# Mixer C: the rounded weight copies move from ScalarE to GpSimd

## The chip, the cores and the metric

The kernel runs on one core of one Trainium2 chip. The core's engines run side by side, each with its own instruction queue, in order: TensorE (PE, with its weight loads as PEld), VectorE (DVE), ScalarE (ACT), GpSimd (POOL) and SyncE (SP), which issues most DMAs. The metric is the device time of one execution in microseconds; smaller is better. Times of several runs are compared by their median.

## The reference

One inference step of a two-layer backbone on 128 context and 1024 latent tokens, 1152 in all, 1024 wide. The even layer has a windowed attention and a bidirectional recurrence side by side; the odd layer, mixer C, is differential attention with 8 heads:

```
h = rms_norm(x, norm_pre) * (1.0 + scale) + shift
qc, kc, vc, gc = split_cols(h @ w_in, ...)        # 8 heads of 128 columns each
p = softmax(q . k / 8)  for both halves of a head # keys: context cache and latent tokens
att = p[0] - lam * p[1]
o = rms_norm(att @ v, subln) * (1.0 - lam_init)
y = (o * silu(gc)) @ w_out
x = x + gate * rms_norm(y, norm_post)
```

Context tokens see context tokens only. Outputs are both token groups and new caches. Everything is fp32.

## The kernel before, in words

To keep fp32 accuracy with TensorE's rounded fp32 format, each operand of a matmul is held as a rounded copy (`hi`) and the remainder (`lo` = value minus `hi`), and a product is three matmuls: hi by hi, lo by hi, hi by lo. For weights this is `load_split` (L265): for each tile of `step` columns SyncE loads `raw` by DMA (L269), ScalarE writes the rounded copy `hi` (L270), and GpSimd writes `lo` = `raw` - `hi` (L271). `weights` (L379) makes the two buffers and calls it.

In the layer of mixer C the tokens lie in nine tiles of 128. For each head h, `c_project` (L1491) loads the head's projection weights `wc` (1024 x 384, six tiles of 128 x 512, buffers `wch` and `wcl`), then for each token tile does 24 matmuls (L360 with `wch`, L361 with `wcl`, L362 with `wch` and the tokens' remainder), rotates q and k (VectorE makes `ropea` and `ropeb`, GpSimd adds them to q and k, L407), casts v, and turns k by a TensorE transpose (L1519) into the key buffer `kst`. `c_probs` makes a token tile's scores `s` (L1555), their minimum `mx` over the negated scores on VectorE (L1557, L1559), the exponentials `p` on ScalarE (L1562) and the difference of the two halves on VectorE (L1575). `c_values` turns that difference (L1593), splits it into `ah` (ScalarE) and `al` (VectorE) and multiplies by v (L1603 to L1605). `c_query` turns and splits q into `qs` (L1533, L1535, L1536). `c_gate` is the gate path (L1620 to L1622), with gate weights `wg` (1024 x 128, two tiles of 128 x 512) that `gate_weights` (L1772) loads; `c_norm` normalizes and multiplies by the gate.

The heads overlap: while head h attends, `ahead` projects head h + 1. Its last part, the first 19 steps of the head after that (`EARLY`), is begun in the last group of head h. There is one buffer of `wch` and one of `wcl` (pool `wc`, one buffer), so a new head's copies wait until TensorE has done the last projection matmul of the head before. There are two buffers of `raw` in the layer (pool `rc`), which also carry the cached keys and values. Head 0's weights are loaded earlier, while the even layer ends, from other `raw` buffers. The generators are interleaved by `zipped` and `run`, and the framework's scheduler then sets the order of each engine's queue by its own costs; the program's text gives the priorities. An engine takes its instructions in that order and waits at each for its inputs.

Of the kernel before, what the change touches and what calls it, by code (L numbers as in the profile page):

```python
# [19 lines left out]
P = 128  # L20
D = 1024
KT = D // P
NT = 9
TOK = NT * P
THIRD = 384
# [116 lines left out]
def hybrid_step(ctx: ExitStack, tc: tile.TileContext, I, O, stop=99):  # L142
    nc = tc.nc
    PE, VE, AE, GE, SP = nc.tensor, nc.vector, nc.scalar, nc.gpsimd, nc.sync
# [7 lines left out]
    def space(name, bufs, **kw):  # L152
        return tc.tile_pool(name=name, bufs=bufs, reuse_waits="tile", **kw)
# [3 lines left out]
    def tl(pool, shape, tag, dt=F32, bufs=None):  # L157
        uid[0] += 1
        kw = {} if bufs is None else {"bufs": bufs}
        return pool.tile(list(shape), dt, tag=tag, name=f"{tag}_{uid[0]}", **kw)  # L160
# [101 lines left out]
        VE.scalar_tensor_tensor(y, t, 1.5, y, op0=ALU.add, op1=ALU.mult)  # L262
        return y

    def load_split(src, hi, lo, n, raw_pool, step=1024, eng=GE):  # L265
        for j in range(0, n, step):
            w = min(step, n - j)
            raw = tl(raw_pool, [P, step], "raw")
            SP.dma_start(raw[:, :w], src[:, j:j + w])  # L269
            AE.copy(hi[:, j:j + w], raw[:, :w])  # L270
            eng.tensor_tensor(lo[:, j:j + w], raw[:, :w], hi[:, j:j + w].bitcast(F32), ALU.subtract)  # L271


# [83 lines left out]
    def proj_steps(ps, hh, hl, wh, wl, t, n):  # L357
        s = slice(P * t, P * t + P)
        for k in range(KT):
            PE.matmul(ps[:, :n], hh[:, k, s], wh[:, k], start=k == 0, stop=False)  # L360
            PE.matmul(ps[:, :n], hh[:, k, s], wl[:, k], start=False, stop=False)  # L361
            PE.matmul(ps[:, :n], hl[:, k, s], wh[:, k], start=False, stop=k == KT - 1)  # L362
            yield
# [12 lines left out]
                PE.matmul(ps[:, :THIRD], wl[:, k], hh[:, k, s], start=False, stop=k == KT - 1)  # L376
            yield i, ps

    def weights(pool, src, n, tag, raw_pool, step=1024, bufs=None):  # L379
        hi, lo = (tl(pool, [P, KT, n], tag + e, F32R, bufs) for e in "hl")  # L380
        load_split(src.rearrange("p k n -> p (k n)"), hi.rearrange("p k n -> p (k n)"),
                   lo.rearrange("p k n -> p (k n)"), KT * n, raw_pool, step)
        return hi, lo

    def rope_apply(pool, rope, ps, n, t, outs):


        w = 64 * n
        m = n // len(outs)
        twice = lambda v, i: v[:, 64 * m * i:64 * m * i + 64 * m].rearrange("p (h o d) -> p h o d", o=1, d=64).to_broadcast(  # L390
            [P, m, 2, 64])
        if t is None:
            for i, out in enumerate(outs):
                AE.copy(out, twice(ps, i))
            return
        cos, sin = rope[:, 0, t], rope[:, 1, t]
        a, b = tl(pool, [P, w], "ropea"), tl(pool, [P, w], "ropeb")
        VE.tensor_tensor(a.rearrange("p (h d) -> p h d", d=64), ps[:, :w].rearrange("p (h d) -> p h d", d=64),
                         cos.rearrange("p (o d) -> p o d", o=1).to_broadcast([P, n, 64]), ALU.mult)
        pv = ps[:, :w].rearrange("p (h c s d) -> p h c s d", c=2, s=2, d=16)  # L400
        bv = b.rearrange("p (h c s d) -> p h c s d", c=2, s=2, d=16)
        sv = sin.rearrange("p (o c s d) -> p o c s d", o=1, c=2, s=2)
        for s in range(2):
            VE.tensor_tensor(bv[:, :, :, s], pv[:, :, :, 1 - s], sv[:, :, :, s].to_broadcast([P, n, 2, 16]),  # L404
                             ALU.mult)
        for i, out in enumerate(outs):
            GE.tensor_tensor(out, twice(a, i), twice(b, i), ALU.add)  # L407
# [15 lines left out]
    def stack_split(dst, src):  # L423
        AE.copy(dst, src)
        VE.tensor_tensor(dst[64:], src[64:], dst[64:].bitcast(F32), ALU.subtract)
# [269 lines left out]
    with ExitStack() as ph1:  # L695
# [35 lines left out]
        rp = ph1.enter_context(space("rp", 2))  # L731
        wq = ph1.enter_context(space("wq", 2))
        wp = ph1.enter_context(space("wp", 2))
# [28 lines left out]
    class Out:  # L762
# [6 lines left out]
        def load_first(s, pool, raw=None, eng=VE):  # L769

            for k in range(4):
                if k in (0, 3):
                    tag, n = ("wg", P) if k else ("wc", THIRD)
                    views = [tl(pool, [P, KT, n], tag + e, F32R).rearrange("p k n -> p (k n)") for e in "hl"]
                hi, lo = (v[:, D * (k % 3):D * (k % 3) + D] for v in views)
                s.w.append((hi, lo))
                for c in (0, 512):
                    load_split(I["wo"][s.l][:, k, c:c + 512], hi[:, c:c + 512], lo[:, c:c + 512], 512, raw or s.raw, 512,
                               eng)
                    yield  # L780

        def load(s, n):

            k0 = len(s.w)
            p = s.pools.enter_context(space(f"ow{s.l}{k0}", 1, side="right"))
            for k in range(k0, k0 + n):
                hi, lo = tl(p, [P, D], f"wo{k}h", F32R), tl(p, [P, D], f"wo{k}l", F32R)
                load_split(I["wo"][s.l][:, k], hi, lo, D, s.raw, 512, VE)
                s.w.append((hi, lo))
# [482 lines left out]
    with ExitStack() as ph2:  # L1272
        bc = ph2.enter_context(space("bc", 1))
        pool = ph2.enter_context(space("bpool", 1))
        last = ph2.enter_context(space("b2", 1))
        early = ph2.enter_context(ExitStack())
        first = ph2.enter_context(ExitStack())
# [91 lines left out]
        for i in range(-2, len(items)):  # L1369
# [16 lines left out]
            if i + 2 == len(items):  # L1386
                run(mod, 1, None, 1)
                first.close()
                wp = late.enter_context(space("wc", 1, side="right"))
# [47 lines left out]
    def split(hi, lo, src):  # L1437
        AE.copy(hi, src)  # L1438
        VE.tensor_tensor(lo, src, hi.bitcast(F32), ALU.subtract)  # L1439
# [7 lines left out]
    def c_open(h, hd, rp, ap):  # L1447

        hd.kst = tl(ap, [P, 2, TOK], "kst", F32R)
        hd.sums = tl(ap, [P, 2 * NT], "sums")  # L1450
        hd.vh, hd.vl = tl(ap, [P, NT, P], "vh", F32R), tl(ap, [P, NT, P], "vl", F32R)
        hd.kp = tl(ap, [P, 2, P], "kp", F32R, 1)
        hd.vph, hd.vpl = tl(ap, [P, P], "vph", F32R, 1), tl(ap, [P, P], "vpl", F32R, 1)
        raw = tl(rp, [P, 512], "raw")
        kr, vr = raw[:, 0:2 * P].rearrange("p (z n) -> p z n", z=2), raw[:, 2 * P:3 * P]
        SP.dma_start(kr, I["ckT"][h])
        SP.dma_start(vr, I["cv"][:, h])
        stack_split(hd.kst[:, :, 0:P], kr)
        split(hd.vh[:, 0], hd.vl[:, 0], vr)
# [30 lines left out]

    def c_project(h, hd, hh, hl, wp, rp, ap, psum, rope):  # L1491
        p_pr, p_tr, p_s, p_o = psum
        wh, wl = weights(wp, I["wc"][h], THIRD, "wc", rp, 512)
        c_open(h, hd, rp, ap)
        yield
        keys = None
        for t in range(NT):
            ps = tl(p_pr, [P, 512], "ps")
            for i, _ in enumerate(proj_steps(ps, hh, hl, wh, wl, t, THIRD)):
                if i == KDEL and keys:  # L1500
                    keys()
                yield
            q, k = tl(ap, [P, 2, 2, 64], "q", bufs=10), tl(ap, [P, 2, 2, 64], "k")
            rope_apply(ap, rope, ps, 4, None if t == 0 else t - 1, (q, k))
            hd.q[t] = q
            if t == 0:
                v = tl(rp, [P, 512], "raw")[:, :P]
                VE.tensor_copy(v, ps[:, 256:384])
                for z in range(2):
                    SP.dma_start(O["ck"][:, h, 64 * z:64 * z + 64], k[:, z, 0])  # L1510
                SP.dma_start(O["cv"][:, h], v)
                split(hd.vph, hd.vpl, v)
            else:
                split(hd.vh[:, t], hd.vl[:, t], ps[:, 256:384])

            def keys(t=t, k=k):
                pt = tl(p_tr, [P, 2, P], "pt")
                for i in range(2):
                    PE.transpose(pt[:, i], k[:, i].rearrange("p o d -> p (o d)"), ident)  # L1519
                stack_split(hd.kp if t == 0 else hd.kst[:, :, P * t:P * t + P], pt)  # L1520

            yield
        for _ in range(KDEL):
            yield
        keys()
        yield
# [153 lines left out]
    with ExitStack() as ph3:  # L1680
# [79 lines left out]
        rp = ph3.enter_context(space("rc", 2))  # L1760
# [4 lines left out]
        heads = [Head() for _ in range(8)]  # L1765

        def project(h):
            if h == 0:
                return c_restore(heads[0], rp, ap, psum)
            return c_project(h, heads[h], hh, hl, wp, rp, ap, psum, rope) if h < 8 else None  # L1770

        def gate_weights(h):  # L1772
            heads[h].wg = weights(wp, I["wgc"][h], P, "wg", rp, 512)

        def gates(h):
            gate_weights(h)
            for _ in range(9):
                yield
            for i in range(3):
                yield from c_gate(i, heads[h], hh, hl, ap, psum)  # L1780
# [28 lines left out]
        first = w1.load_first(wp, rp, GE)  # L1809
# [78 lines left out]
```

## Time and profile before

| what | us |
|---|---|
| median of 3 runs (lowest, highest) | 2082.01 (2075.63, 2087.13) |
| span of the profiled execution | 2077.4 |
| TensorE busy, of the span | 1952.1 |
| VectorE busy | 1488.3 |
| ScalarE busy | 1058.8 |
| GpSimd busy | 673.6 |

The page gives no time around the span. The stretch of mixer C in which the heads' weights are made is about 1170 to 1895 us of the span. A timeline row reads: start, length, engine, line, operation, output from inputs, shape, count, and in brackets how long the engine was idle before it and what ended that idle time. In a row of one source line the three numbers are minimum, median and maximum in ns.

### The profile page before, as it was taken

How to read it: one execution, taken by the hardware profiler on the slowest of the kernel's cores; microseconds unless marked ns; L12 is line 12 of the kernel's file. 1: busy time of each engine (PE TensorE's matmuls, PEld its weight loads, DVE VectorE, ACT ScalarE, POOL GpSimd, SP SyncE). 2: the span in 40 equal slices, each digit the busy share in tenths (PEclk: the TensorE clock that was granted, in tenths of full speed). 3: DMA queues.
4: the chain of work that ended last, by engine and by line, in shares of the span. 5: the costliest groups of instructions: out<-in, count | busy, mean ns of one | idle time of the engine just before them, and what ended most of it. 6: DMA issues, size and time to landing. Idle time of an engine off the chain costs nothing. (4 is left out here: it accounts for less than half of the span.)

```text
span 2077.4 us, 40804 instructions
## 1 busy us (share of the span) xinstructions
PE 1952.1 (94%) x15148; PEld 1777.4 (86%) x15148; DVE 1488.3 (72%) x3821; ACT 1058.8 (51%) x2808; POOL 673.6 (32%) x951
## 2 busy tenths in 40 slices
PE   7899999999789999999989999999999999999998
PEld 7899999999678888777768888999998989898786
DVE  5355567565767787877488587878787878787867
ACT  4343345333446555564356554565555555555643
POOL 0222232332167657575043223121312121212204
PEclk9999999999999999999999999999999999999999
DMA  7511133112555454534576401010101010101325
GB/s 290 163 62 65 61 98 115 63 57 78 181 178 158 146 171 148 157 111 129 167 228 218 133 21 45 15 50 10 51 9 55 6 56 5 55 5 49 106 68 177
DMA packets 165079, 205.72 MB, mean 99 GB/s; under 512 B 16368, under 2 KB 108048, under 8 KB 164880
## 3 DMA queue, kind: packets, MB, share of 16 engines
q1 hardware_dynamic: 162016, 198.25, 30.1%
q10 hardware_dynamic: 2864, 4.85, 0.7%
q8 instruction: 120, 1.97, 0.4%
q14 instruction: 79, 0.65, 0.1%
HBM read 152.32 MB, written 50.74 MB: 98 GB/s over the span
## 5 line engine op out<-in xcount | busy, mean ns | idle before, releaser
L1562 ACT ACTIVATE p<-s,mx 128x384 f32<-128x384 f32 (+1 forms) x400 | 225.1, 572 | 123.0 <-DVE mx L1559 100.3
L1557 DVE TENSOR_REDUCE mc<-s 128x1 f32<-128x384 f32 x384 | 204.4, 551 | 29.3 <-PE s L1555 26.2
L1555 PE MATMUL s<-kst,qs 128*128 128x384 f32 x768 | 196.0, 355 | 14.1 <-ACT p L1562 13.6
L360 PE MATMUL ps<-wch,hh 128*128 128x384 f32 x576 | 205.5, 358 | 3.0 <-DMA raw<-in_wgc_dram 0.9
L361 PE MATMUL ps<-wcl,hh 128*128 128x384 f32 x576 | 198.6, 345 | 4.1 <-POOL wcl L271 4.1
L362 PE MATMUL ps<-wch,hl 128*128 128x384 f32 x576 | 196.4, 341 | 0.3 <-DVE hl L1707 0.2
L407 POOL TENSOR_TENSOR q<-ropea,ropeb 128x256 f32<-128x256 f32 x56 | 44.0, 786 | 442.4 <-DVE ropeb L404 302.3
L374 PE MATMUL ps<-hh,wgh 128*128 128x384 f32 x504 | 174.5, 346 | 5.8 <-DVE bo L242 4.3
L376 PE MATMUL ps<-hh,wgl 128*128 128x384 f32 x504 | 172.4, 342 | 0.0
L375 PE MATMUL ps<-hl,wgh 128*128 128x384 f32 x504 | 171.9, 341 | 0.0
L1555 PEld LDWEIGHTS s<-kst,qs 128*128 128x128 f32 x768 | 127.5, 190 | 29.8 <-ACT p L1562 22.4
L271 POOL TENSOR_TENSOR wgl<-raw,wgh 128x1024 fp32r<-128x1024 f32 (+1 forms) x39 | 75.5, 1939 | 234.5 <-ACT wgh L270 234.5
L1083 POOL TENSOR_TENSOR rp<-rp,tmp 128x126 f32<-128x126 f32 (+22 forms) x279 | 130.3, 467 | 21.9
L1081 POOL TENSOR_TENSOR tmp<-mp,rp 128x126 f32<-128x126 f32 (+22 forms) x279 | 117.8, 422 | 52.3 <-DVE mp L1072 31.1
L1438 ACT CAST ah<-pt 128x512 fp32r<-128x512 f32 (+2 forms) x168 | 86.1, 533 | 79.7 <-PE pt L1593 76.3
L1439 DVE TENSOR_TENSOR al<-pt,ah 128x512 fp32r<-128x512 f32 (+2 forms) x168 | 100.6, 615 | 32.1 <-ACT ah L1438 30.8
L360 PEld LDWEIGHTS ps<-wch,hh 128*128 128x128 f32 x576 | 109.6, 191 | 6.5 <-DVE vl L1439 2.4
L361 PEld LDWEIGHTS ps<-wcl,hh 128*128 128x128 f32 x576 | 109.8, 191 | 6.2 <-POOL wcl L271 5.8
L362 PEld LDWEIGHTS ps<-wch,hl 128*128 128x128 f32 x576 | 109.5, 190 | 1.4 <-DVE hl L1707 1.3
L271 POOL TENSOR_TENSOR wcl<-raw,wch 128x512 fp32r<-128x512 f32 x54 | 76.5, 1423 | 84.5 <-ACT wch L270 84.5
L374 PEld LDWEIGHTS ps<-hh,wgh 128*128 128x128 f32 x504 | 95.4, 189 | 8.1 <-DVE bo L242 4.9
L1575 DVE SCALAR_TENSOR_TENSOR p<-p,lr,p 128x1152 f32<-128x1152 f32 (+1 forms) x72 | 98.4, 1367 | 0.4
(463 smaller groups left out, 5721.7 us busy)
## 6 DMA issues: line engine op xcount, KB each, us to landing
hb<-pbT SPq DMA_DIRECT2D x90, 256.0 KB, 3.9
adaw<-in_ada_w_dram SPq DMA_DIRECT2D x56, 256.0 KB, 3.6
raw<-in_wc_dram SPq DMA_DIRECT2D x48, 256.0 KB, 2.7
adaw<-in_ada_w_dram SPq DMA_DIRECT2D x8, 1024.0 KB, 10.9
pbT<-bm SPq DMA_DIRECT2D x16, 512.0 KB, 2.7
low<-lowT SPq DMA_DIRECT2D x16, 512.0 KB, 4.1
raw<-in_wo_dram SPq DMA_DIRECT2D x32, 256.0 KB, 2.8
raw<-in_wpb_dram SPq DMA_DIRECT2D x13, 512.0 KB, 3.4
```

The costliest lines, as they stand in the source:

```text
L271: eng.tensor_tensor(lo[:, j:j + w], raw[:, :w], hi[:, j:j + w].bitcast(F32), ALU.subtract)
L360: PE.matmul(ps[:, :n], hh[:, k, s], wh[:, k], start=k == 0, stop=False)
L361: PE.matmul(ps[:, :n], hh[:, k, s], wl[:, k], start=False, stop=False)
L362: PE.matmul(ps[:, :n], hl[:, k, s], wh[:, k], start=False, stop=k == KT - 1)
L374: PE.matmul(ps[:, :THIRD], wh[:, k], hh[:, k, s], start=k == 0, stop=False)
L375: PE.matmul(ps[:, :THIRD], wh[:, k], hl[:, k, s], start=False, stop=False)
L376: PE.matmul(ps[:, :THIRD], wl[:, k], hh[:, k, s], start=False, stop=k == KT - 1)
L1081: eng.tensor_tensor(tv, m[:, j - a:j - a + 1, 0:j].to_broadcast([P, n, j]), rpb[:, t:16, j:j + 1].to_broadcast([P, n, j]), ALU.mult)
L1083: eng.tensor_tensor(rpb[:, t:16, 0:j], rpb[:, t:16, 0:j], tv, ALU.add)
L1555: PE.matmul(s[c][:, :w], qs[:, e, z], hd.kp[:, z] if own else hd.kst[:, z, w * c:w * c + w], start=e == 0, stop=e == 1)
L1557: VE.tensor_reduce(mc[:, c:c + 1] if nb > 1 else mx, s[c][:, :w], axis=AX.X, op=ALU.min)
L1562: AE.activation(e[:, w * c:w * c + w], s[c][:, :w], AF.Exp, scale=-1.0, bias=mx, accum_out=sums[:, z, c:c + 1])
```

## The change

`load_split` and `weights` take a function `first` that writes the rounded copy; without it ScalarE does so as before. The projection weights of heads 1 to 7 and the gate weights of heads 1 to 7 are given `GE.tensor_copy`, GpSimd's copy.

```
-    def load_split(src, hi, lo, n, raw_pool, step=1024, eng=GE):
+    def load_split(src, hi, lo, n, raw_pool, step=1024, eng=GE, first=None):
...
-            AE.copy(hi[:, j:j + w], raw[:, :w])
+            (first or AE.copy)(hi[:, j:j + w], raw[:, :w])
...
-    def weights(pool, src, n, tag, raw_pool, step=1024, bufs=None):
+    def weights(pool, src, n, tag, raw_pool, step=1024, bufs=None, first=None):
...
-                   lo.rearrange("p k n -> p (k n)"), KT * n, raw_pool, step)
+                   lo.rearrange("p k n -> p (k n)"), KT * n, raw_pool, step, first=first)
...
-        wh, wl = weights(wp, I["wc"][h], THIRD, "wc", rp, 512)
+        wh, wl = weights(wp, I["wc"][h], THIRD, "wc", rp, 512, first=GE.tensor_copy)
...
-            heads[h].wg = weights(wp, I["wgc"][h], P, "wg", rp, 512)
+            heads[h].wg = weights(wp, I["wgc"][h], P, "wg", rp, 512, first=GE.tensor_copy)
```

The scheduler also sets a new order on TensorE, VectorE and ScalarE; SyncE's is unchanged. Three places, all where head 3's projection weights (`wch_16697`, `wcl_16698`) take the place of head 2's, in the order of the instructions, with - for before and + for the change. On GpSimd:

```order
 L407 TENSOR_TENSOR q_16349<-ropea_16351,ropeb_16352 128x256
 L407 TENSOR_TENSOR k_16350<-ropea_16351,ropeb_16352 128x256
+L270 CAST wch_16697<-raw_16699 128x512
+L270 CAST wch_16697<-raw_16703 128x512
 L271 TENSOR_TENSOR wcl_16698<-raw_16699,wch_16697 128x512
 L271 TENSOR_TENSOR wcl_16698<-raw_16703,wch_16697 128x512
 L407 TENSOR_TENSOR q_16439<-ropea_16441,ropeb_16442 128x256
 L407 TENSOR_TENSOR k_16440<-ropea_16441,ropeb_16442 128x256
+L270 CAST wch_16697<-raw_16707 128x512
 L271 TENSOR_TENSOR wcl_16698<-raw_16707,wch_16697 128x512
```

Two copies stand ahead of the two subtractions and so ahead of the rotated q and k (`k_16440`) of the last token tile of the head before; the other four stand each ahead of its own subtraction. On ScalarE at the same place:

```order
 L424 CAST kst_15384<-pt_16416 128x2x128
-L270 CAST wch_16697<-raw_16699 128x512
-L270 CAST wch_16697<-raw_16703 128x512
 L1438 CAST vh_15386<-ps_16360 128x128
 L1625 ACTIVATE gt_16465<-ps_16426 128x384
-L270 CAST wch_16697<-raw_16707 128x512
 L1438 CAST ah_16474<-pt_16469 128x512
 L1438 CAST ah_16483<-pt_16478 128x512
-L270 CAST wch_16697<-raw_16711 128x512
 L424 CAST kst_15384<-pt_16490 128x2x128
 L1535 ACTIVATE qs_16522<-pt_16519 128x256
-L270 CAST wch_16697<-raw_16715 128x512
```

The copies stood between the casts of turned attention (`ah`), keys and queries; those now follow one another. On TensorE at that place, with the scores `s_3090` and `s_3091` and the transpose of `k_16440`:

```order
-L1622 MATMUL ps_16495<-hh_12964,wgl_15804 128x384
-L1555 MATMUL s_3090_16500<-kst_14181,qs_16330 128x384
 L1603 MATMUL po_16468<-ah_16474,vh_14183 128x256
 L1604 MATMUL po_16468<-ah_16474,vl_14184 128x256
-L1555 MATMUL s_3090_16500<-kst_14181,qs_16330 128x384
-L1555 MATMUL s_3091_16501<-kst_14181,qs_16330 128x384 x2
+L1622 MATMUL ps_16495<-hh_12964,wgl_15804 128x384
+L1555 MATMUL s_3090_16500<-kst_14181,qs_16330 128x384 x2
 L1605 MATMUL po_16468<-al_16475,vh_14183 128x256
 L1519 MATMUL pt_16490<-cst_61,k_16440 128x128 x2
+L1555 MATMUL s_3091_16501<-kst_14181,qs_16330 128x384 x2
```

The value matmuls that read `ah` and the transpose of k stand two to four matmuls earlier than before, and a score block that stood ahead of them now stands behind.

## The prediction

> **What bounds the kernel now.** I read the page first, then the busy times by stretch, then the groups of the stretch in which the change acts, and last the timelines of single places.
>
> ```profile
> PE 1952.1 (94%) x15148; PEld 1777.4 (86%) x15148; DVE 1488.3 (72%) x3821; ACT 1058.8 (51%) x2808; POOL 673.6 (32%) x951
> ```
>
> The page's first part: the columns are busy time, share of the span, count. TensorE is busy for 94% of the span and ScalarE for half of it, so taking work off ScalarE pays only where TensorE waits for it. One head of mixer C repeats about every 102 us, and this is its row:
>
> ```profile
> 1353.00:1455.00 102.00, 99.75 (x637) 94.15 (x637) 82.56 (x235) 58.68 (x176) 24.04 (x24) 1.00 0.10 31
> ```
>
> The columns are length, then busy time of TensorE, its weight loads, VectorE, ScalarE and GpSimd, then the granted clock, the DMA share and GB/s. TensorE is idle for 2.25 of 102 us at full clock. ScalarE has 43 us to spare in it, GpSimd 78. The groups of the stretch 1170 to 1830 us, where seven heads' weights are made, say who ends TensorE's idle time (the last column), and what the moved work costs now:
>
> ```profile
> L361 PE MATMUL ps<-wcl,hh 128*128 128x384 f32 x468 | 161.7, 345 | 4.1 <-POOL wcl L271 4.1
> L1555 PE MATMUL s<-kst,qs 128*128 128x384 f32 x607 | 155.9, 354 | 10.1 <-ACT p L1562 9.5 <-ACT qs L1535 0.5
> L1603 PE MATMUL po<-ah,vh 128*128 128x256 f32 x216 | 70.4, 326 | 2.4 <-ACT ah L1438 2.3
> ...
> L271 POOL TENSOR_TENSOR wcl<-raw,wch 128x512 fp32r<-128x512 f32 x42 | 59.4, 1420 | 73.8 <-ACT wch L270 73.8
> ...
> L270 ACT CAST wch<-raw 128x512 fp32r<-128x512 f32 x42 | 25.4, 623 | 14.5 <-DMA raw<-in_wc_dram 14.4
> ```
>
> So what can be won here is at most 10.1 + 4.1 + 2.4 = 16.6 us of TensorE's idle time, 0.8% of the kernel. What can be lost is not bounded in that way.
>
> **The change part by part.** 42 copies of projection weights (seven heads, six tiles) and 14 of gate weights (seven heads, two tiles) go from ScalarE to GpSimd. ScalarE sheds 56 x 0.623 = 34.9 us of work and, more important, 14.5 us during which its whole queue stood behind a copy whose DMA had not landed. GpSimd gains 56 copies. No SyncE instruction moves. The price of one copy on GpSimd is not in the trace; the nearest row is a copy of the same length per lane on a quarter of the partitions:
>
> ```profile
> L1067 POOL COPY hb<-za x36: 599/610/1007, 578.7 to 946.7; 32x512 f32<-32x512 f32 x36
> ```
>
> It takes 0.61 us (minimum, median, maximum in ns). Above stands the two-input subtraction of 128x512, 1.42 us on average in the group row. I take 0.61, since the length per lane is the same and the input count too; 0.60 and 1.42 stay as ends. The Trainium skill ("GPSIMD Engine Reference", 4.1 Engine selection) calls GpSimd about twice as slow as VectorE for two inputs and roughly line-rate for one input; at its 1.2 GHz and one element a cycle that would be an estimated 0.43 us, and by it k below would come up to 0.36 us earlier at each of six switches, 2.2 us in all. The measured row is slower than the rule; the row is used.
>
> A GpSimd copy does not run undisturbed beside VectorE:
>
> ```profile
> 578.70 3.28 POOL L1067 COPY hb<-za 32x512 f32<-32x512 f32 x4 [14.91 <-DVE za L1040]
> ...
> 579.41 1.08 DVE L988 TENSOR_TENSOR hb<-hb,hb 128x512 f32<-128x512 f32 x1
> 580.52 0.98 DVE L990 TENSOR_TENSOR kbt<-hb,hb 128x512 f32<-128x512 f32 x1
> ```
>
> Four copies took 3.28 instead of 4 x 0.61 = 2.44 us, while VectorE operations on two SBUF operands ran beside them at 1.0 to 1.1 us. I charge this nothing on average, because VectorE has 19 us to spare in a head, and keep it for a rival.
>
> Head 1 (its projection weights are the first that move). The six DMAs begin, the first copy, the first and last subtraction and TensorE's two waits are these:
>
> ```profile
> 1178.65 14.48 SPq L269 DMA_DIRECT2D raw<-in_wc_dram  x6
> 1183.36 0.61 ACT L270 CAST wch<-raw 128x512 fp32r<-128x512 f32 x1
> 1184.04 1.28 POOL L271 TENSOR_TENSOR wcl<-raw,wch 128x512 fp32r<-128x512 f32 x1 [20.20 <-ACT wch L270]
> 1196.51 2.35 POOL L271 TENSOR_TENSOR wcl<-raw,wch 128x512 fp32r<-128x512 f32 x1 [0.24 <-ACT wch L270]
> 1196.33 0.44 PE L361 MATMUL ps<-wcl,hh 128*128 128x384 f32 x1 [0.56 <-POOL wcl L271]
> 1198.91 0.44 PE L361 MATMUL ps<-wcl,hh 128*128 128x384 f32 x1 [1.63 <-POOL wcl L271]
> ```
>
> ```profile
> raw<-in_wc_dram SPq DMA_DIRECT2D x48, 256.0 KB, 2.7
> ```
>
> Here the copies stood between exponentials in ScalarE's queue. On GpSimd a tile takes 0.61 + 1.28 = 1.89 us; with two raw buffers and 2.7 us for a DMA, two tiles take the longer of 3.8 and 1.9 + 2.7 = 4.6. From 1183.4 the fifth tile is done at 1183.4 + 9.2 + 1.9 = 1194.5 and the sixth at 1196.4, against 1198.9 now. TensorE asks for the fifth at 1195.8. Both waits go: **-2.2 us**.
>
> Head 2 is the only other one in which TensorE needs the new weights at once:
>
> ```profile
> 1267.92 1.16 ACT L270 CAST wch<-raw 128x512 fp32r<-128x512 f32 x2
> 1268.64 2.51 POOL L271 TENSOR_TENSOR wcl<-raw,wch 128x512 fp32r<-128x512 f32 x2 [3.52 <-ACT wch L270]
> 1273.67 0.69 PE L1519 MATMUL pt<-cst,k 128*128 128x128 f32 x2 [1.85 <-POOL k L407]
> 1284.32 0.44 PE L361 MATMUL ps<-wcl,hh 128*128 128x384 f32 x1 [0.58 <-POOL wcl L271]
> ```
>
> The copies can begin when TensorE has left the old weights, at 1267.9 in both kernels. Now the subtraction follows 0.72 us later; then it follows two copies, 1.22 us later. All that GpSimd has behind it, the two subtractions and the rotated q and k, is **0.5 us later**, and TensorE waits for k. The third to sixth copies no longer stand behind ScalarE's `ah`, so the 0.58 at 1284 goes. Sum -0.1.
>
> Heads 3 to 7. TensorE has gate matmuls to do and asks for the new weights at 1377, some 19 us after the first copy, so the chain of copies is hidden. What counts is the queue behind them:
>
> ```profile
> 1358.18 1.14 ACT L270 CAST wch<-raw 128x512 fp32r<-128x512 f32 x2
> 1363.48 1.07 ACT L1438 CAST ah<-pt 128x512 fp32r<-128x512 f32 x2
> 1369.00 0.59 ACT L1562 ACTIVATE p<-s,mx 128x384 f32<-128x384 f32 x1
> 1358.87 3.69 POOL L271 TENSOR_TENSOR wcl<-raw,wch 128x512 fp32r<-128x512 f32 x2 [4.10 <-ACT wch L270]
> 1363.23 0.72 POOL L407 TENSOR_TENSOR k<-ropea,ropeb 128x256 f32<-128x256 f32 x1
> 1364.11 0.39 PE L1603 MATMUL po<-ah,vh 128*128 128x256 f32 x1 [0.58 <-ACT ah L1438]
> 1365.11 0.38 PE L1519 MATMUL pt<-cst,k 128*128 128x128 f32 x2
> 1369.73 0.62 PE L1555 MATMUL s<-kst,qs 128*128 128x384 f32 x2 [0.41 <-ACT p L1562]
> 1377.31 0.34 PE L360 MATMUL ps<-wch,hh 128*128 128x384 f32 x1
> ```
>
> With no copy ahead of it, `ah` comes about 1 us earlier and the 0.58 goes. But k, done at 1363.95 now, is done at 1364.5, and the new order has TensorE at the k transpose (L1519) about 1.1 us earlier than 1365.1: it would wait about 0.5 there. Likewise p comes some 0.7 us earlier, but the new order asks for its score matmul five matmuls, about 0.7 us, earlier. I book **0** for these five heads.
>
> Gate weights. Here ScalarE's queue stands behind a DMA, worst in the later heads:
>
> ```profile
> 1602.88 0.62 ACT L270 CAST wgh<-raw 128x512 fp32r<-128x512 f32 x1 [1.47 <-DMA raw<-in_wgc_dram]
> 1604.34 0.58 ACT L1562 ACTIVATE p<-s,mx 128x384 f32<-128x384 f32 x1 [0.56 <-DVE mx L1559]
> 1603.81 0.42 DVE L1536 SCALAR_TENSOR_TENSOR qs<-pt,qs 128x256 fp32r<-128x256 f32 x1 [1.32 <-ACT qs L1535]
> 1605.06 0.61 PE L1555 MATMUL s<-kst,qs 128*128 128x384 f32 x2 [0.60 <-ACT p L1562]
> 1707.88 0.61 PE L1555 MATMUL s<-kst,qs 128*128 128x384 f32 x2 [0.47 <-ACT p L1562]
> 1812.15 0.62 PE L1555 MATMUL s<-kst,qs 128*128 128x384 f32 x2 [1.31 <-ACT p L1562]
> ```
>
> The copy waits 1.47 for its data, `qs` behind it is late, VectorE idles 1.32 for `qs`, and its `mx`, ScalarE's `p` and TensorE's scores follow. With the copy gone the chain starts 1.3 us earlier, more than the wait at its end. The three waits go, 0.60 + 0.47 + 1.31: **-2.4 us**. What is late next is the second score matmul of the pass, 5 us on, whose wait on `p` I leave as it is.
>
> Sum: -2.2 - 0.1 - 2.4 = -4.7 us. The span of the profiled execution is 2077.4; the page gives no time around it, and the median of the three runs, 2082.0, is 4.6 above. 2082.0 - 4.7 gives **2077 us**.
>
> **The rivals.** *More goes:* every wait of TensorE on ScalarE or the subtraction here goes, the 16.6 us above: 2065. For it: ScalarE sheds 5 us in each head. Against it: most of the 10.1 us belongs to `p` behind VectorE's `mx`, which the change does not touch.
>
> *GpSimd becomes the late one, slower:* two copies stand ahead of k in six switches. If collisions with VectorE stretch a copy to the 1.42 us of the upper end, k is late by 2 x 1.42 - 0.7 = 2.1 instead of 0.5 us, six times 1.6 = 10 us. It decides from about 2 us of idle time at one place, since then the clock falls too; head 2 shows it after its 1.85 us wait:
>
> ```profile
> 1274.00:1276.00 2.00, 2.00 (x10) 1.90 (x9) 0.85 (x3) 1.12 (x3) 0.00 (x0) 0.50 0.03 8
> 1276.00:1278.00 2.00, 2.00 (x10) 2.00 (x9) 1.20 (x2) 1.61 (x4) 1.35 (x2) 0.50 0.00 0
> 1278.00:1280.00 2.00, 2.00 (x14) 2.00 (x13) 0.05 (x1) 0.59 (x3) 1.21 (x1) 0.75 0.40 128
> ```
>
> Half clock from 1274 to 1278 and three quarters to 1280 cost about 2.5 us; in five further heads 12 us. 2077 + 10 + 12 gives 2099. Against it: the copy row with its collisions is 0.82 us, and k has slack in the new order only by half a microsecond, so a small loss is likelier than this large one. The Trainium skill ("TensorE: Matmul & The Clock Gate", Part 1) puts the fall to half rate after an idle window of about 3.4 us and the return after as long a busy one; by that rule a new wait of 1 to 2 us alone costs no clock, and this rival would be 2087; the trace fell with 1.85 us after several shorter waits.
>
> *Nothing arrives:* the waits that go are replaced by equal waits on VectorE or k: 2082. And the change may not act: the order shows all 56 moved, head 0's eight copies not, so I give that nothing.
>
> **How the numbers follow.** Forecast 0.60 (own range 2070 to 2085: the sum, with half the median's gap to its extremes), more goes 0.20, slower 0.13, nothing arrives 0.07. A measurement tells about 0.5%, 10.4 us, from no change: faster is below 2071.6, slower above 2092.4. Faster: 0.20 and 0.04 of the forecast's low end; slower 0.13; the rest, 0.63, same. The range reaches from the first rival's 2065 to 2090, leaving out most of the slow rival and a little of the first.
>
> **What would show it.** Copies on GpSimd near 0.61 us, more with collisions; no wait on `wcl` near 1197; no wait for `p` in the gate part of the later heads; a wait on k of about 0.5 us at each switch in place of that on `ah`. Wrong would be: copies at 1.3 us or above, a clock below 1.00 in heads 3 to 7, or a head's period that moves by more than 1 us from 102.

## The result and the profile after

| | before | after |
|---|---|---|
| median of 5 runs, us | 2081.1 | 2098.53 |
| lowest and highest, us | 2075.63, 2087.13 | 2094.12, 2100.48 |
| profiled execution: time | not given | 2098.53 |
| profiled execution: span, us | 2077.4 | 2096.7 |

The ratio of after to before is 1.0063, with a 95% interval from 1.0041 to 1.0085: some 13 us slower. The two medians lie 17.4 us apart; against the 79 later runs of before, with medians of 2083.5 to 2084.8, 2098.53 is 1.0066 to 1.0072, inside the interval, so the ratio is used below. The forecast was 2077, its range 2065 to 2090; the time lies outside.

The first line of the page of the changed kernel, to be held against the one of before:

```profile
PE 1970.8 (94%) x15148; PEld 1794.0 (86%) x15148; DVE 1510.0 (72%) x3821; ACT 1026.7 (49%) x2752; POOL 697.7 (33%) x1007
```

The change did what it says: ScalarE has 56 instructions and 32 us less, GpSimd 56 and 24 us more. What nobody moved has grown as well: VectorE by 21.7 us and TensorE by 18.7 us, with the same instructions. Of TensorE's 18.7, though, 13.7 lie ahead of head 1's first moved copy (1097.7 and 1111.4 us busy up to there), where the change does nothing; of VectorE's 21.7, 20.1 lie behind it. TensorE's groups in the stretch 1170 to 1830 us, and the moved copy:

```profile
L361 PE MATMUL ps<-wcl,hh 128*128 128x384 f32 x463 | 159.1, 344 | 2.4 <-POOL wcl L271 2.4
L1555 PE MATMUL s<-kst,qs 128*128 128x384 f32 x588 | 150.2, 357 | 10.3 <-ACT p L1562 9.7 <-ACT qs L1535 0.5
L1593 PE MATMUL pt<-cst,p 128*128 128x128 f32 x439 | 72.2, 278 | 7.4 <-DVE p L1575 6.6
L1603 PE MATMUL po<-ah,vh 128*128 128x256 f32 x216 | 70.6, 327 | 0.1
L270 POOL CAST wch<-raw 128x512 fp32r<-128x512 f32 x42 | 25.3, 611 | 44.2 <-DMA raw<-in_wc_dram 25.1 <-PE ps L362 18.9
```

The copy takes 0.611 us, as forecast. The wait of L1603 on `ah` is gone (2.4 to 0.1), and L361 lost 1.7. But L1593 now waits 7.4 us on the probability difference `p` of VectorE (1.7 before), and the waits of L1555, from which 2.4 us were to go, are 10.3 as ever. Two places in a head make this.

**The gate part**, where a head's gate weights are split, here in head 4: GpSimd, VectorE and TensorE.

```profile
1616.51 0.61 POOL L270 CAST wgh<-raw 128x512 fp32r<-128x512 f32 x1 [3.96 <-DMA raw<-in_wgc_dram]
1617.20 1.28 POOL L271 TENSOR_TENSOR wgl<-raw,wgh 128x512 fp32r<-128x512 f32 x1
1618.43 0.61 POOL L270 CAST wgh<-raw 128x512 fp32r<-128x512 f32 x1
1619.12 1.28 POOL L271 TENSOR_TENSOR wgl<-raw,wgh 128x512 fp32r<-128x512 f32 x1
...
1616.63 0.51 DVE L250 TENSOR_TENSOR rst<-rsy 128x3 f32<-128x3 f32 x1
1617.37 1.14 DVE L252 SCALAR_TENSOR_TENSOR rsy<-rst,rsy 128x3 f32<-128x3 f32 x1
1618.54 0.52 DVE L250 TENSOR_TENSOR rst<-rsy 128x3 f32<-128x3 f32 x1
1619.45 0.98 DVE L251 SCALAR_TENSOR_TENSOR rst<-rst,vss 128x3 f32<-128x3 f32 x1
...
1623.49 0.83 PE L1555 MATMUL s<-kst,qs 128*128 128x384 f32 x2 [2.10 <-ACT p L1562]
```

The four VectorE rows belong to the inverse square root of the head's norm (`rsqrt`, L247 to L252): three numbers a lane, 0.16 us each when nothing is beside them. Compare ends: 1616.63 + 0.51 = 1617.14 with the first copy's 1617.12; 1617.37 + 1.14 = 1618.51 with the subtraction's 1618.48; 1619.06 with 1619.04; 1620.43 with 1620.40. Each of these four VectorE instructions ends 0.02 to 0.03 us after the GpSimd instruction beside it. In VectorE's queue the minima L1557 and `mx` L1559 stand between and behind them, ScalarE's `p` waits for `mx`, TensorE for `p`. In before the same place has two stretched instructions, for only two subtractions ran there, 3.1 us apart:

```profile
1604.40 0.48 DVE L1643 TENSOR_SCALAR vss<-vss 128x3 f32<-128x3 f32 x1
1606.99 1.03 DVE L252 SCALAR_TENSOR_TENSOR rsy<-rst,rsy 128x3 f32<-128x3 f32 x1
```

The Trainium skill ("SBUF — State Buffer", SBUF: two separate sides) describes this as an exclusive lock on a port pair that VectorE and GpSimd share, held for the whole instruction; which instruction comes first has it, and the other blocks fully. It says so of VectorE instructions in a two-port mode or with two inputs from SBUF, as the four above have. Their ends, 0.02 to 0.03 us apart, agree. The stretched L1643 has one input from SBUF and was held as well: 1604.40 + 0.48 = 1604.88, 0.02 us behind the end of a subtraction. No run shows whether it counts as such a mode.

**The switch** to the next projection weights, 40 us ahead of that place:

```profile
1575.90 2.54 POOL L271 TENSOR_TENSOR wcl<-raw,wch 128x512 fp32r<-128x512 f32 x2
1576.19 1.02 DVE L1574 SCALAR_TENSOR_TENSOR lr<-lr,nlam,sums 128x1 f32<-128x1 f32 x1
1577.34 2.32 DVE L1575 SCALAR_TENSOR_TENSOR p<-p,lr,p 128x1152 f32<-128x1152 f32 x1
1579.71 0.99 PE L1593 MATMUL pt<-cst,p 128*128 128x128 f32 x7 [1.20 <-DVE p L1575]
```

L1574 is held under the first subtraction, L1575 under the second, and TensorE waits 1.20 us for it. Undisturbed, L1575 takes 1.41 us (the median of its rows in both kernels). At the same switch in before it came earlier and was held by the first subtraction alone, 2.00 us:

```profile
1562.66 3.68 POOL L271 TENSOR_TENSOR wcl<-raw,wch 128x512 fp32r<-128x512 f32 x2 [4.11 <-ACT wch L270]
1563.19 2.00 DVE L1575 SCALAR_TENSOR_TENSOR p<-p,lr,p 128x1152 f32<-128x1152 f32 x1
```

There the second subtraction waited for L1575, so that the pair took 3.68 us and not 2.54.

**The clock.** Granted clock around the longest wait of head 3, in the eighth column (length, busy times of the five engines, clock, DMA):

```profile
1515.00:1518.00 3.00, 0.84 (x5) 0.53 (x4) 2.75 (x13) 0.92 (x3) 0.01 (x1) 0.99 0.30 85
1518.00:1523.00 5.00, 5.00 (x23) 4.96 (x23) 2.75 (x9) 2.07 (x9) 1.42 (x2) 0.67 0.00 0
1523.00:1528.00 5.00, 5.00 (x29) 4.48 (x29) 4.88 (x12) 3.23 (x12) 0.00 (x0) 1.00 0.01 2
```

After a wait of 2.16 us TensorE runs at a mean of two thirds for 5 us, which is 5 x 0.33 = 1.65 us of work lost. Three of the six gate waits (2.16, 2.10 and 1.99 us) are followed by this, the others (1.64, 1.37, 1.53) are not.

**Not of the change.** Up to mixer C both kernels have the same instructions in the same order, yet head 1's first copy of `wch` begins at 1183.4 us before and at 1191.4 after. In twelve profiles with the same order up to there (before, after and the ten below) it begins between 1183.4 and 1192.1, and the granted clock up to there differs too, 0.98 before and 0.97 after. So single profiles are compared below from that copy to the end of the span: 894.0 us before (1183.4 to 2077.4), 905.3 after (1191.4 to 2096.7), **11.3 us more**. A tail still holds the clock's luck of one execution, some us either way.

### The profile page after: what moved, and what is told of

The parts are those of the page before. It is cut to its first block, busy times and chain, and to the rows that moved or that the text cites. A ratio compares the mean times of both kernels' runs of the same rounds, so it can differ in the third digit from the quotient of the medians.

```text
span 2096.7 us, 40789 instructions
## 1 busy us (share of the span) xinstructions
PE 1970.8 (94%) x15148; PEld 1794.0 (86%) x15148; DVE 1510.0 (72%) x3821; ACT 1026.7 (49%) x2752; POOL 697.7 (33%) x1007
## 5 line engine op out<-in xcount | busy, mean ns | idle before, releaser
L1557 DVE TENSOR_REDUCE mc<-s 128x1 f32<-128x384 f32 x384 | 204.8, 552 | 53.2 <-PE s L1555 50.2
L1555 PE MATMUL s<-kst,qs 128*128 128x384 f32 x768 | 195.5, 357 | 15.7 <-ACT p L1562 15.2
L407 POOL TENSOR_TENSOR q<-ropea,ropeb 128x256 f32<-128x256 f32 x56 | 50.6, 904 | 464.4 <-DVE ropeb L404 374.1
L361 PE MATMUL ps<-wcl,hh 128*128 128x384 f32 x576 | 197.6, 343 | 2.4 <-POOL wcl L271 2.4
L1555 PEld LDWEIGHTS s<-kst,qs 128*128 128x128 f32 x768 | 129.2, 192 | 30.1 <-ACT p L1562 22.6
L361 PEld LDWEIGHTS ps<-wcl,hh 128*128 128x128 f32 x576 | 110.5, 192 | 3.8 <-POOL wcl L271 3.6
L1593 PE MATMUL pt<-cst,p 128*128 128x128 f32 x584 | 95.4, 277 | 8.3 <-DVE p L1575 6.6
L1575 DVE SCALAR_TENSOR_TENSOR p<-p,lr,p 128x1152 f32<-128x1152 f32 (+1 forms) x72 | 99.9, 1387 | 0.4
```

What stands on the lines that cost most here:

```text
L1555: PE.matmul(s[c][:, :w], qs[:, e, z], hd.kp[:, z] if own else hd.kst[:, z, w * c:w * c + w], start=e == 0, stop=e == 1)
L1557: VE.tensor_reduce(mc[:, c:c + 1] if nb > 1 else mx, s[c][:, :w], axis=AX.X, op=ALU.min)
```

## The experiments

Theory A: GpSimd's instructions hold up small VectorE instructions that run beside them, and the price is paid where those are on TensorE's path. Rival B: the loss is the new order that the scheduler set on TensorE, VectorE and ScalarE. Rival C: the loss lies ahead of mixer C. All kernels were timed in 5 rounds; the line numbers in some shift by up to 9. The last column is the time from head 1's first copy to the end in each profile.

| kernel | median, us | ratio to before (95%) | tail, us |
|---|---|---|---|
| before | 2081.1 | | 894.0 |
| after | 2098.53 | 1.0063 (1.0041, 1.0085) | 905.3 |
| e1 only `wc` moved | 2079.29 | 0.9981 (0.9967, 0.9995) | 887.1 |
| e2 only `wg` moved | 2098.33 | 1.0062 (1.0042, 1.0082) | 906.5 |
| e3 after, `wg` copies held | 2088.95 | 1.0026 (1.0012, 1.0040) | 900.8 |
| e4 before, `wg` subtractions held | 2096.73 | 1.0059 (1.0036, 1.0082) | 903.4 |
| e5 e1, `wg` subtractions behind k | 2079.53 | 0.9978 (0.9964, 0.9991) | 890.7 |
| e6 before, the same | 2086.09 | 1.0014 (0.9998, 1.0031) | 895.4 |
| e7 after, rotation behind L1575 | 2098.32 | 1.0066 (1.0045, 1.0086) | 908.6 |
| e8 e3, one `wc` subtraction held too | 2084.42 | 1.0000 (0.9988, 1.0013) | 893.3 |
| e9 after, L1660 behind L1559 | 2090.51 | 1.0038 (1.0023, 1.0053) | 900.5 |
| e10 e3 and e9 together | 2084.29 | 1.0001 (0.9984, 1.0018) | 893.2 |

The runs of before that were made beside each set had medians of 2084.8 (e1 to e4), 2083.5 (e5 to e8) and 2084.3 us (e9, e10); the ratios are to these.

### One half of the change each

e1 takes the second line of the change back, e2 the first:

```
e1: heads[h].wg = weights(wp, I["wgc"][h], P, "wg", rp, 512)
e2: wh, wl = weights(wp, I["wc"][h], THIRD, "wc", rp, 512)
```

> Only the copies of the projection weights wc are on GpSimd; the gate weights' copies are back on ScalarE. Theory A (GpSimd's new instructions hold up small VectorE instructions that run at the same time; the price is paid where those lie on TensorE's path, most of it beside the head's norm while the gate weights are split): the waits of L1555 on p in the gate part are as before, 0.7 to 1.0 us a head, and no half clock follows; the wait of L1593 on p of L1575 at the switch stays at 1.2 us as in the changed kernel. Time 2081 + 5 x 0.6 = about 2084. Rival B (the scheduler's new order is the loss): this kernel's VectorE order is near that of before, so 2081. Rival C (the loss is in the early stages, which this change does not touch): about 2090 to 2098 or no pattern, and the profile loses time ahead of 1160 us.

> Only the copies of the gate weights wg are on GpSimd; the projection weights' copies are back on ScalarE. Theory A: the gate part's waits of L1555 on p are 1.4 to 2.2 us a head in heads 3 to 7, with the clock below 1.00 for some us behind the longest; the switch has the old wait on ah, about 0.6. Time 2081 + 5 x (0.6 to 1.2) + 3 x 1.5 = 2088 to 2092. Rival B: VectorE's order here differs from that of the changed kernel in few rows, so the same 2090 to 2098. Rival C: no pattern.

The whole loss comes with the gate weights, 14 of the 56 copies: moved alone, with the order that the scheduler then sets, they are as slow as the change. The projection weights alone gain 0.19%, so e1 beats both kernels. Its groups in 1170 to 1830 us:

```profile
L361 PE MATMUL ps<-wcl,hh 128*128 128x384 f32 x474 | 163.4, 345 | 2.3 <-POOL wcl L271 2.3
L1555 PE MATMUL s<-kst,qs 128*128 128x384 f32 x608 | 155.1, 354 | 7.6 <-ACT p L1562 7.1 <-ACT qs L1535 0.5
L1593 PE MATMUL pt<-cst,p 128*128 128x128 f32 x447 | 73.0, 277 | 1.0
L1603 PE MATMUL po<-ah,vh 128*128 128x256 f32 x217 | 70.7, 326 | 0.1
```

Against before, the idle time is 1.8 + 2.5 + 0.7 + 2.3 = 7.3 us less; the tail is 6.9 less. The times did not speak for theory A: e1, at 0.9981 of 2081.1 or 2077, lies below both theories' 2084 and 2081, and e2, at 1.0062 or 2094, lies in rival B's range and above theory A's. In the trace theory A was wrong on e1 in one thing: the wait of 1.2 us at the switch is not there. It appears in e2 (1.01 to 1.03), where no projection copy was moved. So it is not these copies that make it, and the order has a part in it. C falls: the loss goes with an edit in mixer C alone.

### The collision in the gate part, undone

e3 makes GpSimd's gate copies wait for the last VectorE instruction of the norm's chain. TensorE, VectorE and ScalarE keep the order of the change, row by row.

```
-            (first or AE.copy)(hi[:, j:j + w], raw[:, :w])
+            c = (first or AE.copy)(hi[:, j:j + w], raw[:, :w])
+            if hold is not None:
+                tc.add_manual_dep(c.ins, hold.ins.name, mybir.DependencyInfo(
+                    mybir.DependencyClass.Sync, mybir.DependencyReason.DATA), reason="hold")
...
-        VE.tensor_tensor(rs, rs, il, ALU.mult)
+        hd.normed = VE.tensor_tensor(rs, rs, il, ALU.mult)
...
-                gate_weights(h)
+                gate_weights(h, heads[h - 1].normed)
```

> The changed kernel, with GpSimd's copies of the gate weights made to wait until VectorE has done the last instruction of the norm's chain (L1645). The order on TensorE, VectorE and ScalarE is that of the changed kernel, instruction by instruction; on GpSimd the two subtractions stand two rows later. Theory A: L250 to L252 in the gate part are all near 0.16 us, mx is ready about 2 us sooner, the waits of L1555 on p fall from 1.4 to 2.2 us to below 0.7 us and no half clock follows them: 2098 less 5 x 1.2 less 3 x 1.5 = about 2088. Rival B: the order is the same, so 2098. Rival C: 2098.

Time and mechanism came as theory A had them: 1.0063 falls to 1.0026 with the same order. In head 4 of e3:

```profile
1612.79 0.15 DVE L251 SCALAR_TENSOR_TENSOR rst<-rst,vss 128x3 f32<-128x3 f32 x1
1613.93 1.17 POOL L270 CAST wgh<-raw 128x512 fp32r<-128x512 f32 x2 [8.69 <-DVE rsy L1648]
1618.60 0.62 PE L1558 MATMUL s<-kst,qs 128*128 128x384 f32 x2 [0.45 <-ACT p L1565]
```

The chain runs at 0.15 to 0.16 us an instruction, the wait of 2.10 is 0.45, and all stretches of 100 us from 1300 to 1800 show clock 1.00. This part is worth 1.0063 - 1.0026 = 0.0037 of the kernel, 7.7 us, with intervals of 0.0022 and 0.0014 to either side of the two ratios. Rival B alone can't make that, for nothing was reordered but two rows of GpSimd.

e4 adds the same wait to the kernel before, whose two gate subtractions also collide; every queue keeps its order.

```
-            eng.tensor_tensor(lo[:, j:j + w], raw[:, :w], hi[:, j:j + w].bitcast(F32), ALU.subtract)
+            c = eng.tensor_tensor(lo[:, j:j + w], raw[:, :w], hi[:, j:j + w].bitcast(F32), ALU.subtract)
+            if hold is not None:
+                tc.add_manual_dep(c.ins, hold.ins.name, mybir.DependencyInfo(
+                    mybir.DependencyClass.Sync, mybir.DependencyReason.DATA), reason="hold")
```

> The kernel before, with nothing changed but one added wait: GpSimd's subtractions of the gate weights in heads 1 to 6 wait for the last VectorE instruction of the norm's chain (L1645). The order on every engine is that of before. Theory A: the two stretched instructions of the chain (L1643 at 0.48, L252 at 0.98 to 1.03) shrink to 0.15 us, and the waits of L1555 on p in the gate part (0.7 to 1.0 us) shrink by as much: 2081 less 5 x 0.9 = about 2077, which is faster than both. Rival B: no change, 2081. Rival C: no change, 2081.

All three missed: 12 us slower. The collision did go, and a worse wait took its place:

```profile
1620.24 2.53 POOL L271 TENSOR_TENSOR wgl<-raw,wgh 128x512 fp32r<-128x512 f32 x2 [9.28 <-DVE rsy L1648]
1622.74 0.74 POOL L410 TENSOR_TENSOR q<-ropea,ropeb 128x256 f32<-128x256 f32 x1
1623.45 1.83 POOL L410 TENSOR_TENSOR k<-ropea,ropeb 128x256 f32<-128x256 f32 x1
1625.34 0.44 PE L1522 MATMUL pt<-cst,k 128*128 128x128 f32 x2 [2.06 <-POOL k L410]
```

The held subtractions stand ahead of q and k in GpSimd's queue, so k is late and TensorE waits 2 us for it in each of six heads. I had named the wait, and not what is queued behind it. In e3 the scheduler had put the subtractions behind q and k itself.

So e5 and e6 put them there without a wait, by an order rule on GpSimd alone, in e1 and in before:

```
-            eng.tensor_tensor(lo[:, j:j + w], raw[:, :w], hi[:, j:j + w].bitcast(F32), ALU.subtract)
+            behind(eng.tensor_tensor(lo[:, j:j + w], raw[:, :w], hi[:, j:j + w].bitcast(F32), ALU.subtract), [late])
...
-            GE.tensor_tensor(out, twice(a, i), twice(b, i), ALU.add)
+            turned_k[0] = GE.tensor_tensor(out, twice(a, i), twice(b, i), ALU.add)
...
-                gate_weights(h)
+                gate_weights(h, turned_k[0])
```

> The kernel of the projection weights alone (their copies on GpSimd, the gate weights' copies on ScalarE), and GpSimd's two subtractions of the gate weights stand behind the next q and k in GpSimd's queue instead of ahead of them, with no added wait. The order on TensorE, VectorE and ScalarE is that kernel's. Theory A (a GpSimd instruction holds up small VectorE instructions of the norm's chain, and through VectorE's queue p): no stretched instruction in the chain, the waits of L1555 on p fall from 0.7 to 1.0 us to below 0.4 us, and k is not late, since q and k now stand ahead: 0.3% below the kernel of the projection weights alone, ratio to before about 0.995 to 0.996. Rival B (only the order on TensorE, VectorE and ScalarE counts): as that kernel, 0.998.

> The kernel before, all copies on ScalarE; only the two subtractions of the gate weights stand behind the next q and k in GpSimd's queue, without the wait that the held variant had. Order on TensorE, VectorE and ScalarE as before. Theory A: the waits of L1555 on p lose 0.5 to 0.9 us in five to six heads and the wait of 2.06 us on k that the held variant had is absent: 4 us below before, ratio 0.998. That the held subtractions cost time only by standing ahead of k is right if so. Rival B: ratio 1.000. If holding costs by something else, the ratio stays at 1.005.

The wait on k is gone, which confirms the reading of e4, and the waits on `p` fell to 0.34 to 0.39 us as expected, yet no time was won: e5 is as e1, e6 as before. Head 4 in e5:

```profile
1612.62 2.52 POOL L273 TENSOR_TENSOR wgl<-raw,wgh 128x512 fp32r<-128x512 f32 x2
1613.23 0.69 DVE L1576 SCALAR_TENSOR_TENSOR lr<-lr,nlam,sums 128x1 f32<-128x1 f32 x1
1613.96 2.40 DVE L1577 SCALAR_TENSOR_TENSOR p<-p,lr,p 128x1152 f32<-128x1152 f32 x1
1617.34 0.33 PE L1595 MATMUL pt<-cst,p 128*128 128x128 f32 x1 [0.47 <-DVE gt L1662]
```

The subtractions now hold up the pass's combination instead of its norm, and TensorE waits 0.47 us for a product behind it. Six such waits of 0.46 us on average, 2.8 us, take back most of the 3.3 us that the six waits on `p` lost (5.5 in e1, 2.2 here). VectorE is busy for 80% of the time here, and the collision that was moved found another victim. That is why theory A, though right about the mechanism, offered less in these two than I expected of it.

### The switch

e7 puts the rotation's two instructions L404 behind L1575 again, as in before, in the changed kernel (VectorE only, heads 2 to 7).

```
-            VE.tensor_tensor(bv[:, :, :, s], pv[:, :, :, 1 - s], sv[:, :, :, s].to_broadcast([P, n, 2, 16]),
-                             ALU.mult)
+            i = VE.tensor_tensor(bv[:, :, :, s], pv[:, :, :, 1 - s], sv[:, :, :, s].to_broadcast([P, n, 2, 16]),
+                                 ALU.mult)
+            if late is not None:
+                behind(i, [late])
```

> The changed kernel; only on VectorE, at the five switches from head 2 on, the two instructions L404 of the last tile stand behind L1575 as they do before, not between L1573, L1574 and L1575. Order on TensorE, ScalarE and GpSimd as in the changed kernel. Theory A (L1575 ends when GpSimd's second subtraction has ended and 1.2 us more, whatever stands ahead of it): L1574 still starts under the first subtraction, so the wait of L1593 on p stays at 1.2 us, ratio to before 1.006. Rival B (order): L1575 starts 0.4 to 0.6 us sooner and the wait falls to 0.6 to 0.8 us, 3 us less, ratio 1.0045.

A was right and so was its time, 1.0066 against 1.006: the wait stayed at 1.17 to 1.20 us. Starting L1575 sooner is worth nothing while the second subtraction runs.

e8 is e3 with, in addition, the first `wc` subtraction of a switch held until VectorE has done L1575.

```
+            if j == 0 and hold_lo is not None:
+                tc.add_manual_dep(c.ins, hold_lo.ins.name, mybir.DependencyInfo(
+                    mybir.DependencyClass.Sync, mybir.DependencyReason.DATA), reason="hold")
```

> The changed kernel with the gate weights' copies held behind the norm's chain (as in the held variant before), and at the switches from head 2 on also the first subtraction of the projection weights held until VectorE has done L1575; GpSimd then does one subtraction, q, k, and the second subtraction. Order on TensorE, VectorE and ScalarE is that of the changed kernel. Theory A: L1574 near 0.2 to 0.6 us (only the two copies may hold it), L1575 at 1.4 us instead of 2.3, and the wait of L1593 falls from 1.20 us to about 0 to 0.3 us: 5 x 1.0 = 5 us less than the held variant, ratio to before 1.000. k is asked 3 us later, so it should not be late. Rival B (order alone): as the held variant, 1.0026.

```profile
1569.12 1.29 POOL L274 TENSOR_TENSOR wcl<-raw,wch 128x512 fp32r<-128x512 f32 x1
1569.30 1.14 DVE L1583 SCALAR_TENSOR_TENSOR lr<-lr,nlam,sums 128x1 f32<-128x1 f32 x1
1570.56 1.40 DVE L1584 SCALAR_TENSOR_TENSOR p<-p,lr,p 128x1152 f32<-128x1152 f32 x1
1572.01 0.44 PE L1602 MATMUL pt<-cst,p 128*128 128x128 f32 x2 [0.40 <-DVE p L1584]
```

L1575 (here L1584) is back at 1.40 and the wait at 0.40 (0 to 0.3 expected); the time came as expected, 1.000. The small instruction ahead stayed long (1.14, expected 0.2 to 0.6), since the other subtraction runs beside it.

What brought L1575 under the second subtraction when e1 has the same copies there? In the order of the change the gate's product L1660 (0.56 us) stands ahead of the maximum `mx` L1559 in the last score pass of a head; so `mx`, `p` and L1571 to L1575 come half a microsecond later against the subtractions. In e2 the pair is turned as well (L1660 at 1568.58, `mx` at 1569.06), in e1 it is not, which fits the wait that e2 has and e1 lacks. e9 turns back this one pair:

```
-                VE.tensor_reduce(mx, mc, axis=AX.X, op=ALU.min)
+                Head.last_mx = VE.tensor_reduce(mx, mc, axis=AX.X, op=ALU.min)
...
-        VE.tensor_tensor(g, pr.rearrange("p a q -> p (a q)"), g, ALU.mult)
+        turned = VE.tensor_tensor(g, pr.rearrange("p a q -> p (a q)"), g, ALU.mult)
+        if 0 < h < 7:
+            behind(turned, [Head.last_mx])
```

> The changed kernel with one pair of VectorE instructions turned back: the gate's L1660 stands behind the maximum L1559 of the last score pass of a head, as before, not ahead of it. From this one rule the scheduler sets L1571 to L1575 and the rotation at the switches of heads 2 to 7 in the order of before; the order on TensorE and ScalarE up to head 7, and on GpSimd, is that of the changed kernel. Theory D (the new order makes p's chain 0.5 us later at the switch, so that L1574 meets GpSimd's first subtraction and L1575 the second): L1574 falls to about 0.5 us and is done when the first subtraction starts, L1575 takes about 2.1 us as in the kernel of the projection weights alone, the wait of L1593 falls from 1.20 to 0 to 0.3 us; the gate part stays as it is, with 1.4 to 2.3 us on p and half clock. 5 to 6 us less than the changed kernel: ratio to before about 1.0035. If the order doesn't matter as long as GpSimd's copies and subtractions lie there: 1.006.

> Both repairs on the changed kernel: the gate weights' copies held until VectorE has done the norm's chain, and L1660 behind L1559 as before. Theory D with theory A: waits of L1558 on p in the gate part near 0.4 us without half clock, no wait of L1596 at the switch. The held variant was 1.0026; 5 us less gives 1.000 or slightly below (0.999). If the two repairs overlap, 1.002.

Both came within 0.0003 of the expected ratio. VectorE and GpSimd at a switch of e9, then VectorE in e1 at the same place:

```profile
1360.56 0.29 DVE L1574 SCALAR_TENSOR_TENSOR lr<-lr,nlam,sums 128x1 f32<-128x1 f32 x1
1361.22 1.41 DVE L1575 SCALAR_TENSOR_TENSOR p<-p,lr,p 128x1152 f32<-128x1152 f32 x1
1361.36 3.68 POOL L271 TENSOR_TENSOR wcl<-raw,wch 128x512 fp32r<-128x512 f32 x2
```

```profile
1363.12 0.54 DVE L1574 SCALAR_TENSOR_TENSOR lr<-lr,nlam,sums 128x1 f32<-128x1 f32 x1
1364.04 2.09 DVE L1575 SCALAR_TENSOR_TENSOR p<-p,lr,p 128x1152 f32<-128x1152 f32 x1
```

Now L1575 is first and undisturbed (2.1 us had been expected, as in e1), and the two subtractions wait for it, 3.68 instead of 2.54 us. The wait of L1593 at the switch is gone. This has a small price: k stands behind the subtractions on GpSimd, and TensorE now waits 0.30 us for it at each of the five switches. This repair is worth 1.0063 - 1.0038 = 0.0025, the gate repair 0.0037; together 0.0062, and e10 measures 1.0063 - 1.0001 = 0.0062. Each ratio has an interval of 0.0014 to 0.0022 to either side, so within that the two causes add up to the loss against before. The single tails agree only roughly: the repairs take 4.8 and 4.5 us off, both together 12.1. The gain that was forecast is not there even so.

What stays open: e10, with both repaired, doesn't reach e1, though 42 + 14 copies have left ScalarE in it against 42. It is not that TensorE waits longer: over five heads, from one gate part's wait to another's, e10 takes 513.1 us (1312.9 to 1826.0) and e1 508.6 (1307.5 to 1816.1), both at clock 1.00, and 3.9 of these 4.5 us are counted as busy time of TensorE. Nor is the new order free of waits: L1533 waits 2.3 us for `al` in the changed kernel, its counterpart in e10 2.2, and in before and e1 it does not wait. So the new order may have a price of its own of about 4 us beside the two collisions, and no run tests it. Why the scheduler turned the pair is open as well.

## Why the prediction was wrong, point by point

- **A copy takes 0.61 us on GpSimd:** right, 0.611 in the median; one of the 56 took 1.74.
- **"I charge this nothing on average, because VectorE has 19 us to spare in a head":** this is the step that failed. The spare time of a whole head says nothing of a chain of a dozen dependent instructions of 0.16 us, with the maximum for the next scores queued behind them. Four GpSimd instructions within 3.9 us stretched four of them by 2.5 us in head 4, where before two had been stretched by 1.2. The collision of the two engines had been seen, but only GpSimd's side of it was kept, as a rival; what it does to VectorE was put at nothing, and that cost 7.7 us in the gate part (e3, which also undoes the collisions that before had there).
- **Gate weights, -2.4:** the three waits of 0.60, 0.47 and 1.31 us did go. But "the second score matmul of the pass, whose wait on `p` I leave as it is" is where it was given back: 0.73 to 0.95 us before, 1.37 to 2.16 after, and half clock behind three of the six. ScalarE's slow copies had spaced GpSimd's subtractions; taking the stall away packed them together.
- **Heads 3 to 7, booked as 0:** the wait on `ah` went as told. The 0.5 us on k did not come; instead L1593 waits 1.20 on L1575, and turning that back is worth 5.2 us in all (e9). I had read the new order on the engines for k and p, and not the pair L1660 and L1559 upstream of both.
- **Head 1, -2.2:** the wait of 1.63 went, one of 0.57 stayed. The stretch from its first copy to head 2's is 83.0 us instead of 84.6. That the copies did this is not shown: before ran from 1183.4 to 1190.2 us at clock 0.50 and after did not, and e4, with ScalarE's copies and clock 1.00 over the whole stretch, takes 82.6. The 2.2 us are not borne out.
- **Head 2, -0.1:** k waits 1.87 (1.85 before), not 0.5 more; the wait of 0.58 at 1284 went, one on `wcl` grew from 0.91 to 1.34.
- **The rival "GpSimd becomes late, slower", 2099:** its time was met by luck, its mechanism was not. It had collisions stretch GpSimd's copies ahead of k; the 42 copies of projection weights stayed at 0.60 to 0.63, and VectorE was the one held up. The fall of the clock after waits near 2 us came as it said.
- **"More goes", 2065:** less than half of it exists, and not in the changed kernel. e1 takes 6.6 of the 16.6 us away, 7.3 with L1593; the wait on `p` behind `mx` stays, as said against it.

Of the 11.3 us in the two tails, 6.2 are idle time of TensorE (39.6 before, 45.8 after) and 5.1 are busy time (854.4 and 859.5). The three stretches at two thirds of the clock cost 5 x (0.33 + 0.31 + 0.30) = 4.7 us. The busy time is a balance, though: before alone lost clock in head 1. What both kernels lost past 1900 us stays open.

## What to carry to other kernels

Before moving work to GpSimd, look for VectorE rows in the trace that are several times as long as their shape warrants and end with a GpSimd instruction: that price is already being paid, and more GpSimd instructions raise it where they run in a row. Charge it at the place and not by spare time per stage, and follow VectorE's queue behind the held instruction. Where a change has two parts, time each alone: here the larger one gains 0.19% and the smaller one costs 0.6%.

## What the hardware showed that I had not expected

- An instruction on three numbers a lane is held as fully as one on 1152: 0.16 us becomes 1.14 beside one GpSimd subtraction. A single-input copy on GpSimd holds too (0.51 us at 1616.63). The minima L1557, which read from PSUM, are not held (mean 551 ns before, 552 after).
- The clock goes in steps, and where a wait lies in them decides. In all twelve profiles the granted clock is 0.50 or 1.00 and changes only at multiples of 3.41 us from its first record. In e4 the same wait of 1.99 to 2.07 us on k occurs six times in one execution. Four times 1.99 to 2.06 us of it lay within one step, and the next step ran at 0.50; twice the edge of a step cut it, into 0.39 and 1.68 or 0.32 and 1.74 us, and the clock stayed at 1.00. First a whole wait and the step behind it, then a cut one in its two steps and the step behind:

```profile
1517.15:1520.56 3.41, 1.35 (x9) 1.03 (x9) 2.47 (x4) 1.80 (x6) 3.05 (x3) 1.00 0.53 154
1520.56:1523.97 3.41, 3.41 (x14) 3.31 (x13) 1.62 (x4) 0.37 (x1) 0.00 (x0) 0.50 0.00 0
1411.34:1414.75 3.41, 3.02 (x18) 2.67 (x16) 3.19 (x10) 1.99 (x9) 3.41 (x4) 1.00 0.23 71
1414.75:1418.16 3.41, 1.73 (x12) 1.70 (x13) 1.73 (x3) 1.41 (x5) 1.63 (x1) 1.00 0.27 82
1418.16:1421.57 3.41, 3.41 (x22) 3.23 (x21) 3.25 (x10) 1.46 (x5) 0.00 (x0) 1.00 0.02 9
```

  The three waits of the changed kernel that cost clock lie in one step each, the other three are shorter. In e9 a wait of 2.09 us was cut into 0.72 and 1.36 and cost none. So a start that is shifted by a microsecond or two changes which waits cost clock as well: this is the clock's luck in a single execution.
- The Trainium skill ("TensorE: Matmul & The Clock Gate", Part 1) puts the fall behind an idle window of about 3.4 us. The length of a step here, 3.41 us, agrees. No wait of TensorE in these stretches was that long, so the measurement decides on the rest: about 2 us of one wait in one step (1.93 in e2) was enough, 1.74 was not.
